# Hybrid retention and short-convolution block: token high and low parts side by side in 512-wide products, part sums by DMA, retention moved behind the input groups

## The chip, the cores and the metric

The kernel runs on one core of one Trainium2 chip. The metric is device time in microseconds (us), the median over several executions; less is better. One more execution was profiled: its trace gives the start and length of each instruction on each engine (TensorE, VectorE, ScalarE, GpSimd and SyncE; in the rows PE for matmuls, PEld for weight loads, DVE, ACT, POOL and SP), the DMA transfers, and the waits.

## The reference, cut to what matters

One layer over 512 tokens with 2048 features, float32:

```python
h = rmsnorm(x, norm_gain)
proj = h @ w_in                       # 2048 x 12288 columns
q, k, v, g_ret, c_b, c_c, c_x, g_conv, merge = split(proj)   # eight times 1024, then 4096
q = rotary(q); k = rotary(k) * 128 ** -0.5                   # 8 heads of 128
o = retention(q, k, v, decay, forward) + retention(q, k, v, decay, backward, strict)
branch_ret = o * rsqrt(mean(o * o) + eps) * gn_gain * silu(g_ret)
branch_conv = c_b * conv3_centred(c_c * c_x, conv_w) * silu(g_conv)
up = branch_ret @ w_branch[0], branch_conv @ w_branch[1]     # each 1024 x 2048
merged = sigmoid(merge[0]) * up[0] + sigmoid(merge[1]) * up[1]
out = rmsnorm(x + merged @ w_out, final_gain)
```

## The kernel before, in words

**Numbers in two parts.** Every float32 matrix is split in a rounded high part and the rest, the low part. `split_to` (L138) makes both: ScalarE copies to the high part (L140), VectorE subtracts (L141). A product is three matmuls (`mm3`, L143): high x high, high x low, low x high, each with its own weight load.

**Groups and pieces.** The columns of `w_in` are cut into 48 groups of 256: four each for k, q, v and g of the retention, 16 for the convolution, 16 for the merge gates. A group is four pieces of 512 KB (four k-tiles of 128 rows by 256 columns). `run` (L156) walks through all pieces in order: it issues the loads three pieces ahead on the SyncE queue, has the piece two ahead split, then emits the matmuls of the piece (`use`) and after that one entry of the list `background`. A piece has three `raw` buffers, three `whi` and two `wlo`, so the low part of piece n+2 can be written only when TensorE is through with piece n. The instructions of the first pieces are kept in program order; after `state["full"]` (L807) a scheduler that builds the program orders each engine's queue by its own estimates, and on the chip each queue then runs in that fixed order.

**Three kinds of input group.** `group` (L171) holds weights still and moves 512 tokens: 96 matmuls of 512 columns. `group_tok` (L277, for v) holds tokens still: 192 matmuls of 256 columns. `group_s` (L197) is a Strassen-Winograd form over 2 x 2 blocks (two halves of the tokens, two k-tiles, two column halves): seven products in place of eight, each of 256 tokens, 168 matmuls of 256 columns a group. Its weight sums are made on VectorE for each piece (`sums`, L134 to L136: one addition of 512 elements, two of 256), so that the pieces that are split have 1792 columns in place of 1024. Its token sums are made once (`token_forms`, L263). Its seven sums lie in four PSUM banks, and `combine` (L247) makes the four blocks from them: one ScalarE copy of 512 elements and four VectorE additions of 512. Two sets of four banks alternate.

**Order.** 12 plain groups and four of `group_tok` for the retention's k, q, v, g, pair of heads by pair of heads; the retention itself (`score`, `outp`, `rms_o`, `finish`) runs as background steps of later pieces, nine slots for a pair of heads. Then three plain gate groups, `token_forms`, 27 groups of `group_s` (16 of the convolution, 11 gates), two plain gate groups; then 16 groups of the two branch projections (1024 rows each, 48 matmuls of 512 columns), alternating, and the output projection. Gates and both branches go through DRAM on the GpSimd queue.

Of the kernel before, what the change touches and what calls it, by code (L numbers as in the profile page):

```python
# [20 lines left out]
H = 8  # L21
# [9 lines left out]
def hybrid_block_kernel(  # L31
# [20 lines left out]
    big = ctx.enter_context(tc.tile_pool(name="big", bufs=2))  # L52
    wp = ctx.enter_context(tc.tile_pool(name="wp", bufs=3))
    WF = 7 * 256
    dr = ctx.enter_context(tc.tile_pool(name="dr", bufs=1, space=bass.MemoryType.DRAM))
    ps = ctx.enter_context(tc.tile_pool(name="ps", bufs=2, space=PSUM))
# [13 lines left out]
    rsp = ctx.enter_context(ExitStack())  # L70
    gate_d = dr.tile([2, KT, P, S], F32, name="gate_d")
    ret_d = dr.tile([GG, P, S], F32, name="ret_d")
    conv_d = dr.tile([GG, P, S], F32, name="conv_d")

# [18 lines left out]
    state = {"loaded": 0, "split": 0, "used": 0, "full": False, "banks": 0}  # L93
# [6 lines left out]
    def load(pc, lo=0, hi=None):  # L100
        a, b = pc["dims"]
        if lo == 0:
            pc["F"] = wp.tile([P, WF], F32, name="raw", tag="raw", bufs=3)
            pc["raw"] = pc["F"][:, : a * b].rearrange("p (a b) -> p a b", a=a)
        pin(nc.sync.dma_start(out=pc["raw"][:, lo:hi], in_=pc["src"][:, lo:hi]))

    def split(pc, lo=0, hi=None):
        a, b = pc["dims"]
        if lo == 0:
            fl = []  # L110
            for n, k in (("whi", 3), ("wlo", 2)):
                if pc.get("last", 8) < 8 - k:
                    fl.append(fin["x"].tile([P, 1024], F32R, name=n, tag=n, bufs=8 - k))
                else:
                    fl.append(wp.tile([P, WF], F32R, name=n, tag=n, bufs=k))
# [8 lines left out]
    def blocks(pc):  # L124

        r = pc["F"][:, :1024].rearrange("p (r h c x) -> p r h c x", r=2, h=2, c=2)
        return r, pc["F"][:, 1024:].rearrange("p (f r x) -> p f r x", f=3, r=2)

    def sums(pc):

        r, s = blocks(pc)
        b21 = r[:, :, 1, 0, :].unsqueeze(2).broadcast_to([P, 2, 2, P])
        diag = pc["F"][:, :1024].rearrange("p (r m x) -> p r m x", r=2, m=4)[:, :, 0:4:3, :]
        nc.vector.tensor_tensor(s[:, 0:2].rearrange("p f r x -> p r f x"), diag, b21, op=ALU.add)  # L134
        nc.vector.tensor_tensor(r[:, :, 1, 0, :], s[:, 0], r[:, :, 1, 1, :], op=ALU.add)
        nc.vector.tensor_tensor(s[:, 2], r[:, :, 1, 0, :], r[:, :, 0, 1, :], op=ALU.add)  # L136
# [14 lines left out]
    def split_upto(n):  # L151
        while state["split"] < min(n, len(pieces)):
# [3 lines left out]
    def run(upto):  # L156
        while state["used"] < upto:
            i = state["used"]
            while state["loaded"] < min(i + 4, len(pieces)):
# [11 lines left out]
    def group(src, nk, rhs, post, mid=None):  # L171

        st = {}
        for q in range(nk // 4):
            def use(pc, q=q):
                if q == 0:
                    st["acc"] = ps.tile([P, 2, S], F32, name="acc", tag="acc")
                wh, wl = pc["w"]
                first = bool(mid) and q == 0
                for n in range(8):  # L180
# [3 lines left out]
                        mm3(  # L184
                            st["acc"][:, j, :],
                            (wh[:, k, c], wl[:, k, c]),
                            (rhs()[0][:, kt, :], rhs()[1][:, kt, :]),
                            kt == 0,
                            kt == nk - 1,
                        )  # L190
# [6 lines left out]
    def group_s(src, post):  # L197


        st = {}  # L200

        order = [
            (0, 0, "b11", "d4"), (0, 1, "b12", "a11"), (1, 1, "b22", "a12"), (2, 0, "v", "a1"),
            (1, 0, "u", "a22"), (3, 0, "z", "a7"), (3, 1, "w", "d6"),
        ]
        seen = [next(i for i, o in enumerate(order) if o[0] == b) for b in range(4)]
        for q in range(KT // 4):
            def use(pc, q=q):
                if q == 0:
                    pool = ps if state["banks"] % 2 == 0 else fin["psS"]  # L210
                    state["banks"] += 1
                    st["acc"] = [pool.tile([P, 2, S], F32, name="acc", tag="acc") for _ in range(2)]
                for n, (bank, half, b, a) in enumerate(order):
                    acc = st["acc"][bank // 2][:, bank % 2, half * 256 : half * 256 + 256]
                    for r in range(2):
                        mm3(
                            acc,
                            [weight_form(w, b, r) for w in pc["w"]],
                            token_form(a, 2 * q + r),
                            q == 0 and r == 0 and n in seen,  # L220
                            q == KT // 4 - 1 and r == 1,
                            skip_group_check=True,
                        )
                if q == KT // 4 - 1:
                    post(combine(*st["acc"]))
            pieces.append({"dims": (4, 256), "src": src[:, 4 * q : 4 * q + 4, :], "use": use, "forms": True})

    def weight_form(w, name, r):
        at = {"b11": 0, "b12": 128, "v": 256, "b22": 384}
        if name in at:  # L230
            o = 512 * r + at[name]
        else:
            o = 1024 + 256 * "uzw".index(name) + 128 * r
        return w[:, o : o + 128]

    def token_form(name, j):
        if name in ("a11", "a12", "a22"):
            kt, t = 2 * j + (name[2] == "2"), 256 * (name[1] == "2")
            return [h[:, kt, t : t + 256] for h in hT]
        i = ("d6", "d4", "a1", "a7").index(name)  # L240
        return [f[:, j, i, :] for f in part["forms"]]

    def swapped(t):

        return bass.AP(t.tensor, t.offset + 256, [t.ap[0], [-256, 2], [1, 256]])

    def combine(x, y):  # L247

        tp = part["tp"]
        t = tp.tile([P, 2, S], F32, name="T", tag="T", bufs=3)  # L250
        flat = t.rearrange("p j (i s) -> p (j i) s", i=2)
        s = tp.tile([P, S], F32, name="sc", tag="sc", bufs=1)
        nc.scalar.activation(s, x[:, 0, :], AF.Copy)
# [648 lines left out]
```

## Time and profile before

| | |
|---|---|
| median of 3 runs | 1443.73 us (1442.91 to 1446.1) |
| the profiled execution | 1444.66 us, of which the trace's span is 1442.8 us |
| TensorE busy | 1423.4 us, 99% of the span |
| VectorE busy | 945.2 us, 66% |
| ScalarE busy | 549.2 us, 38% |
| DMA | 174.93 MB, mean 121 GB/s |
| mean granted TensorE clock | 0.995 of full speed |

Busy time of TensorE is the time in which at least one matmul is under way; matmuls overlap, so the distance between starts, not the length of one, says how fast it goes. An engine's mean share is taken over stages of different kinds, so the stages are read one by one.

### The profile page before, as it was taken

Reading aid. Unit: us, or ns where it says so; the run is one execution under the profiler, and the core shown is the slowest. Engines: PE = TensorE matmul, PEld = TensorE weight load, DVE = VectorE, ACT = ScalarE, POOL = GpSimd, SP = SyncE. Lnnn points to the kernel's source line nnn. Section 1 sums busy time; section 2 is a strip of 40 time slices with the busy share of each in tenths; the row PEclk is TensorE's granted clock in tenths of the full one; section 3 lists DMA queues with packets and bytes.
Section 4 is the critical chain, followed back from the end, with each engine's and each line's share of the span. In section 5 each row is a group of like instructions: output and inputs, shape, how many; then the busy total and the mean of one; then the engine's idle time right before and its main releaser. Section 6 shows DMA issues by size and latency. Waiting matters only on the chain.

```text
span 1442.8 us, 20988 instructions
## 1 busy us (share of the span) xinstructions
PE 1423.4 (99%) x8810; PEld 1286.1 (89%) x8810; DVE 945.2 (66%) x1220; ACT 549.2 (38%) x586; POOL 65.8 (5%) x80
## 2 busy tenths in 40 slices
PE   8999999999999999999999999999999999999997
PEld 7888988988988899999999999999978888888886
DVE  4846557466467989988898899889643444522433
ACT  6435335354344434443344334434342222222421
POOL 0000000000000000000000000000010000201210
PEclk9999999999999999999999999999999999999999
DMA  6322322322323333443344334433464444543412
GB/s 229 94 87 84 107 77 86 102 79 97 102 68 121 117 95 106 140 132 103 103 132 135 100 116 134 132 103 103 148 231 161 146 146 146 186 179 102 162 55 105
DMA packets 140610, 174.93 MB, mean 121 GB/s; under 512 B 5940, under 2 KB 122724, under 8 KB 139876
## 3 DMA queue, kind: packets, MB, share of 16 engines
q1 hardware_dynamic: 132788, 143.17, 30.7%
q0 software_dynamic: 7696, 30.41, 6.3%
q8 instruction: 69, 1.13, 0.3%
q14 instruction: 25, 0.20, 0.0%
q10 hardware_dynamic: 32, 0.01, 0.0%
HBM read 156.79 MB, written 16.78 MB: 120 GB/s over the span
## 4 chain that ended last, share of the span: by engine, by line
PE 92%; DVE 5%; DMA 2%; issue 1%; ACT 0%; SPq 0%; DVEq 0%; ACTq 0%
PE acc L147 29%; PE acc L145 29%; PE acc L146 29%; DVE wlo L141 2%; DMA raw<-in_w_in_dram 1%; PE op L147 1%; PE sp L147 1%; PE sp L145 1%; PE op L145 1%; PE op L146 1%; PE sp L146 1%; DVE raw L134 0%; PE xtp L346 0%; DMA xb<-in_x_dram 0%; DVE fl L141 0%
## 5 line engine op out<-in xcount | busy, mean ns | idle before, releaser
L141 DVE TENSOR_TENSOR wlo<-raw,whi 128x1024 fp32r<-128x1024 f32 (+2 forms) x257 | 402.5, 1568 | 351.0 <-PE acc L147 139.8
L140 ACT ACTIVATE whi<-raw 128x1024 fp32r<-128x1024 f32 (+2 forms) x257 | 339.6, 1326 | 560.1 <-PE acc L146 312.9
L147 PE MATMUL acc<-hTh,wlo 128*128 128x256 f32 (+1 forms) x1192 | 396.0, 332 | 2.4 <-DVE wlo L141 2.4
L145 PE MATMUL acc<-hTh,whi 128*128 128x256 f32 (+1 forms) x1192 | 396.6, 333 | 0.7 <-DVE de L257 0.7
L146 PE MATMUL acc<-hTl,whi 128*128 128x256 f32 (+1 forms) x1192 | 395.9, 332 | 0.0
L147 PEld LDWEIGHTS acc<-hTh,wlo 128*128 128x128 f32 x1192 | 227.0, 190 | 24.9 <-DVE wlo L141 3.3
L147 PE MATMUL acc<-fh,wlo 128*128 128x256 f32 x864 | 245.5, 284 | 2.6 <-DVE wlo L141 2.6
L145 PEld LDWEIGHTS acc<-hTh,whi 128*128 128x128 f32 x1192 | 227.2, 191 | 22.1 <-issue 0.8
L146 PEld LDWEIGHTS acc<-hTl,whi 128*128 128x128 f32 x1192 | 227.1, 191 | 21.2
L145 PE MATMUL acc<-fh,whi 128*128 128x256 f32 x864 | 244.6, 283 | 0.3 <-DVE T L574 0.2
L146 PE MATMUL acc<-fl,whi 128*128 128x256 f32 x864 | 244.5, 283 | 0.0
L147 PEld LDWEIGHTS acc<-fh,wlo 128*128 128x128 f32 x864 | 166.1, 192 | 3.6 <-DVE wlo L141 3.3
L145 PEld LDWEIGHTS acc<-fh,whi 128*128 128x128 f32 x864 | 166.0, 192 | 0.8 <-DVE T L574 0.4
L146 PEld LDWEIGHTS acc<-fl,whi 128*128 128x128 f32 x864 | 166.0, 192 | 0.0
L146 PE MATMUL acc<-wlo,mTh 128*128 128x512 f32 (+1 forms) x272 | 102.5, 377 | 0.0
L147 PE MATMUL acc<-whi,mTl 128*128 128x512 f32 (+1 forms) x272 | 102.5, 377 | 0.0
L145 PE MATMUL acc<-whi,mTh 128*128 128x512 f32 (+1 forms) x272 | 102.5, 377 | 0.0
L145 PE MATMUL acc<-bh,whi 128*128 128x512 f32 x256 | 99.6, 389 | 0.0
L146 PE MATMUL acc<-bl,whi 128*128 128x512 f32 x256 | 99.6, 389 | 0.0
L147 PE MATMUL acc<-bh,wlo 128*128 128x512 f32 x256 | 99.6, 389 | 0.0
L134 DVE TENSOR_TENSOR raw<-raw 128x512 f32<-128x512 f32 x108 | 74.3, 688 | 16.4 <-DMA raw<-in_w_in_dram 16.3
L146 PE MATMUL acc<-wlo,hTh 128*128 128x256 f32 x256 | 72.4, 283 | 0.0
(171 smaller groups left out, 1546.0 us busy)
## 6 DMA issues: line engine op xcount, KB each, us to landing
raw<-in_w_in_dram SPq DMA_DIRECT2D x191, 512.0 KB, 3.6
raw<-in_w_branch_dram SPq DMA_DIRECT2D x32, 512.0 KB, 3.3
raw<-in_w_out_dram SPq DMA_DIRECT2D x32, 512.0 KB, 3.6
gate_d<-T POOLq DMA_DIRECT2D x16, 512.0 KB, 3.8
gl<-gate_d POOLq DMA_DIRECT2D x16, 512.0 KB, 4.4
y<-in_x_dram POOLq DMA_DIRECT2D x4, 1024.0 KB, 6.6
xb<-in_x_dram SPq DMA_DIRECT2D x12, 256.0 KB, 6.4
ret_d<-tmp POOLq DMA_DIRECT2D x8, 256.0 KB, 2.4
```

The source lines that it names most:

```text
L134: nc.vector.tensor_tensor(s[:, 0:2].rearrange("p f r x -> p r f x"), diag, b21, op=ALU.add)
L140: pin(nc.scalar.activation(hi, src, AF.Copy))
L141: pin(nc.vector.tensor_tensor(lo, src, hi.bitcast(F32), op=ALU.subtract))
L145: pin(nc.tensor.matmul(acc, lh, rh, start=start, stop=False, **kw))
L146: pin(nc.tensor.matmul(acc, lh, rl, start=False, stop=False, **kw))
L147: pin(nc.tensor.matmul(acc, ll, rh, start=False, stop=stop, **kw))
```

## The change

- 40 of the 48 input groups use `group_s`: all but the four of k and the four of v. So 13 groups that were plain (four q, four g, five gates) join the 27.
- In a product of `group_s` the high and low parts of the tokens lie side by side: one matmul moves both (512 columns) under the high part of the weights, a second one of 256 columns adds the weights' low part times the tokens' high part. Each product has a PSUM bank of its own, in two halves. In the last piece of a group ScalarE copies each of the seven banks to SBUF (`ev`, one buffer); a DMA on the GpSimd queue then adds the second halves onto the first, and `combine` takes its four additions from there.
- For this the tokens h are stored as three arrays: k-tiles 0 to 7 (`h1`), and k-tiles 8 to 15 in halves of 256 tokens (`h00`, `h10`). Plain groups therefore use two matmuls of 256 for k-tiles 8 to 15. `h10` is written to DRAM before the `group_s` stage, its place is taken by `ev`, and it is read back for the last two v groups.
- Order: k (four groups), v 0 and 1, token forms in the background of these; the 40 groups; then the projections of the convolution branch, with v 2 and 3 among them, with the whole retention as background in 22 slots (27 steps; in five slots two steps come together); then the projections of the retention branch. q, k, v, g and the gated projection of the convolution branch go through DRAM.

```diff
-    order = [(0, 0, "b11", "d4"), (0, 1, "b12", "a11"), (1, 1, "b22", "a12"), ...]
+    order = [
+        ("b11", "d4", 0), ("b12", "a11", 1), ("u", "a22", 2), ("b22", "a12", 3),
+        ("z", "a7", 4), ("w", "d6", 5), ("v", "a1", 6),
+    ]
     for q in range(KT // 4):
         def use(pc, q=q):
             if q == 0:
-                st["acc"] = [pool.tile([P, 2, S], F32, name="acc", tag="acc") for _ in range(2)]
+                tiles = [fin["p7"].tile([P, 2, 256], F32, name="acc", tag="acc") for _ in order]
+                st["acc"] = tiles if state["banks"] else [tiles[i] for i in (4, 5, 6, 2, 3, 0, 1)]
...
                 for r in range(2):
-                    mm3(acc, [weight_form(w, b, r) for w in pc["w"]], token_form(a, 2 * q + r), ...)
+                    wh, wl = [weight_form(w, b, r) for w in pc["w"]]
+                    x = token_form(a, q + 4 * r)
+                    first, last = q == 0 and r == 0, q == KT // 4 - 1 and r == 1
+                    nc.tensor.matmul(acc, wh, x, start=first, stop=False, skip_group_check=True)
+                    nc.tensor.matmul(acc[:, 1, :], wl, x[:, 0], start=False, stop=last, skip_group_check=True)
+                if q == KT // 4 - 1:
+                    nc.scalar.activation(EV()[:, :, place, :], acc, AF.Copy)
             if q == KT // 4 - 1:
-                post(combine(*st["acc"]))
+                sum_parts()
+                if pc.get("defer"):
+                    state["defer"] = lambda: post(combine())
+                else:
+                    post(combine())
+
+def sum_parts():
+    e = EV()
+    nc.gpsimd.dma_start(out=e[:, 0, 0:7, :], in_=e[:, 1, 0:7, :], accum_op=ALU.add)
...
+def combine():
+    e = EV()[:, 0]
+    t = T()
+    flat = t.rearrange("p j (i s) -> p (j i) s", i=2)
+    s, back = e[:, 0:2, :], e[:, 3, :]
+    back = bass.AP(back.tensor, back.offset, [back.ap[0], [-256, 2], [1, 256]])
+    nc.vector.tensor_tensor(flat[:, 1:3, :], s, e[:, 2:4, :], op=ALU.add)
+    nc.vector.tensor_tensor(s, s, back, op=ALU.subtract)
+    m1 = e[:, 6:7, :].broadcast_to([P, 2, 256])
+    nc.vector.tensor_tensor(s, s, m1, op=ALU.add)
+    nc.vector.tensor_tensor(flat[:, 0:4:3, :], s, e[:, 4:6, :], op=ALU.add)
...
 def group(src, nk, rhs, post, mid=None, ahead=None):
...
+                    for t, r in rhs(kt):
+                        mm3(st["acc"][:, j, t : t + r.shape[2]], (wh[:, k, c], wl[:, k, c]), (r[:, 0], r[:, 1]), ...)
...
+others = [(cols(0, i), rotary_post(q_d, i)) for i in range(4)] + [(cols(3 * BW, i), g_post(i)) for i in range(4)]
+others += [(cols(8 * BW, i), gate_post(i)) for i in list(range(8, 16)) + list(range(8))]
 for i in range(BW // 256):
+    for n, (off, post) in enumerate(conv_posts(i)):
+        group_s(cols((4 + off) * BW, i), post)
+        for _ in range((1, 2, 1, 2)[n]):
+            group_s(*others.pop(0))
...
+for n in range(2):
+    up_group(1, n, conv_up_post(n))
+for i in range(2, 4):
+    group_tok(cols(2 * BW, i), v_post(i))
+    up_group(1, i, conv_up_post(i))
+for i in range(4, 8):
+    up_group(1, i, conv_up_post(i))
+n_r = len(pieces)
 for i in range(D // 256):
+    up_group(0, i, ret_up_post(i))
...
+def retention_program():
+    steps = [[] for _ in range(6 * (H // 2) + 3)]
+    for i in range(H // 2):
+        a, b = 2 * i, 2 * i + 1
+        own = [
+            [L(split_v, i), L(split_head, a), L(decay_table, a), L(fetch_head, b)],
+            [L(score, a, 0), L(score, a, 1)],
+            [L(outp, a, 0), L(outp, a, 1), L(score, a, 2), L(score, a, 3), L(fetch_g, a)],
+            [L(outp, a, 2), L(outp, a, 3), L(square, a), L(split_head, b), L(decay_table, b)],
+            [L(score, b, 0), L(score, b, 1), L(rms_o, a)] + ([L(fetch, i + 1), L(fetch_head, a + 2)] if b + 1 < H else []),
+            [L(outp, b, 0), L(outp, b, 1), L(score, b, 2), L(score, b, 3), L(finish, a), L(fetch_g, b)],
+            [L(outp, b, 2), L(outp, b, 3), L(square, b)],
+            [L(rms_o, b)],
+            [L(finish, b)],
+        ]
+        for k, s in enumerate(own):
+            steps[6 * i + k] += s
+    n = 22
+    return [sum(steps[k * len(steps) // n : (k + 1) * len(steps) // n], []) for k in range(n)]
```

`rotary_post`, `g_post` and `v_post` now end in a write to DRAM; `fetch`, `fetch_head` and `fetch_g` read it back into SBUF on the GpSimd queue, `split_head` and `split_v` split it there. The piece of a `group_s` group now takes k-tiles q, q+4, q+8 and q+12, and the token forms lie in four arrays by q, so that each comes free after the piece that uses it last. The load and the split of the convolution branch's tokens stand at the end of the 40 groups, those of the retention branch's after the retention.

## Rows read from the trace of the kernel before

**Rows 1.** The page's first part: busy time, share of the span, instructions.

```profile
PE 1423.4 (99%) x8810; PEld 1286.1 (89%) x8810; DVE 945.2 (66%) x1220; ACT 549.2 (38%) x586; POOL 65.8 (5%) x80
```

**Rows 2.** Busy time by stretch: length, PE, PEld, DVE, ACT, POOL, clock, DMA share, GB/s.

```profile
40.00:240.00 200.00, 200.00 (x1063) 172.65 (x1062) 120.85 (x195) 87.65 (x111) 1.83 (x3) 1.00 0.28 88
240.00:440.00 200.00, 200.00 (x1061) 172.85 (x1060) 112.50 (x150) 85.73 (x110) 2.16 (x4) 1.00 0.28 88
700.00:860.00 160.00, 159.31 (x1325) 158.91 (x1324) 141.21 (x174) 63.52 (x46) 2.85 (x4) 1.00 0.37 116
```

**Rows 3.** The same view of the passage into the `group_s` stage.

```profile
490.00:500.00 10.00, 8.03 (x63) 7.41 (x61) 9.97 (x14) 5.31 (x5) 0.71 (x1) 1.00 0.31 105
500.00:510.00 10.00, 9.93 (x70) 9.93 (x71) 8.39 (x12) 3.41 (x2) 0.00 (x0) 0.83 0.38 115
```

**Rows 4.** Timelines of PE: start, length, matmul; first and last of 53 and 20.

```profile
899.75 0.28 PE L146 MATMUL acc<-fl,whi 128*128 128x256 f32 x1
...
905.99 0.28 PE L147 MATMUL acc<-fh,wlo 128*128 128x256 f32 x1
...
1149.65 0.39 PE L145 MATMUL acc<-bh,whi 128*128 128x512 f32 x1
...
1153.95 0.39 PE L146 MATMUL acc<-bl,whi 128*128 128x512 f32 x1
```

**Rows 5.** Timeline of DVE at a `group_s` group's end: start, length, instruction.

```profile
572.37 0.68 DVE L255 TENSOR_TENSOR T<-sc,acc 128x512 f32<-128x512 f32 x1
572.96 2.02 DVE L141 TENSOR_TENSOR wlo<-raw,whi 128x1792 fp32r<-128x1792 f32 x1
574.90 0.68 DVE L257 TENSOR_TENSOR de<-sc,acc 128x512 f32<-128x512 f32 x1
575.50 0.69 DVE L134 TENSOR_TENSOR raw<-raw 128x512 f32<-128x512 f32 x1
...
576.70 0.42 DVE L135 TENSOR_TENSOR raw<-raw 128x256 f32<-128x256 f32 x1
577.03 0.68 DVE L260 TENSOR_TENSOR T<-de,acc 128x512 f32<-128x512 f32 x1
...
579.57 1.22 DVE L612 TENSOR_TENSOR T<-T,rsrow 128x1024 f32<-128x1024 f32 x1
580.70 0.42 DVE L136 TENSOR_TENSOR raw<-raw 128x256 f32<-128x256 f32 x1
```

**Rows 6.** Groups of instructions, 560 to 860 us: busy, mean; idle before.

```profile
L141 DVE TENSOR_TENSOR wlo<-raw,whi 128x1792 fp32r<-128x1792 f32 x60 | 121.1, 2022 | 16.4 <-PE acc L147 13.8 <-ACT whi L140 2.2
...
L140 ACT ACTIVATE whi<-raw 128x1792 fp32r<-128x1792 f32 x60 | 101.3, 1700 | 106.9 <-DVE raw L136 66.1 <-PE acc L146 35.3 <-PE acc L147 5.5
L253 ACT ACTIVATE sc<-acc 128x512 f32<-128x512 f32 x15 | 8.8, 588 | 15.5 <-PE acc L147 15.5
```

**Rows 7.** DMA issues: size of one, median us to landing.

```profile
gate_d<-T POOLq DMA_DIRECT2D x16, 512.0 KB, 3.8
...
y<-in_x_dram POOLq DMA_DIRECT2D x4, 1024.0 KB, 6.6
```

**Rows 8.** Waits in all (total, times, longest); DVE's timeline where the branches load.

```profile
ACT bh L140 <- DMA bl<-conv_d: 9.5, 4, 3.2
...
1076.83 1.23 DVE L141 TENSOR_TENSOR bl<-bl,bh 128x1024 fp32r<-128x1024 f32 x1 [1.80 <-ACT bh L140]
1077.97 2.35 DVE L141 TENSOR_TENSOR wlo<-raw,whi 128x1024 fp32r<-128x1024 f32 x2
```

**Rows 9.** Timelines of DVE and ACT: what follows two scores.

```profile
92.29 1.28 DVE L481 SCALAR_TENSOR_TENSOR tmp<-sp,tb 128x512 f32<-128x512 f32 x2
93.67 1.29 DVE L141 TENSOR_TENSOR sl<-tmp,sh 128x512 fp32r<-128x512 f32 x2
...
93.01 1.23 ACT L140 ACTIVATE sh<-tmp 128x512 fp32r<-128x512 f32 x2 [0.97 <-DVE tmp L481]
```

**Rows 10.** Groups by line and shape, 40 to 440 us, DVE: one of rotary's three.

```profile
L425 DVE TENSOR_TENSOR tmp<-acc,rot 128x512 f32<-128x512 f32 x16 | 11.0, 690 | 6.4 <-ACT tmp L423 6.4
```

More of the change, by code (lines that the diff above doesn't have):

```diff
@@ L92, in hybrid_block_kernel @@
     fin = {}
-    state = {"loaded": 0, "split": 0, "used": 0, "full": False, "banks": 0}
+    state = {"loaded": 0, "split": 0, "used": 0, "full": False, "banks": 0, "limit": 0}
     def pin(ins):
@@ L151, in split_upto @@
     def split_upto(n):
-        while state["split"] < min(n, len(pieces)):
+        while state["split"] < min(n, state["limit"]):
             split(pieces[state["split"]])
@@ L158, in run @@
             i = state["used"]
-            while state["loaded"] < min(i + 4, len(pieces)):
+            while state["loaded"] < min(i + 4, state["limit"]):
                 load(pieces[state["loaded"]])
@@ L176, in use @@
                 if q == 0:
[L177 removed]
+                    st["acc"] = acc_tile()
+                    if ahead:
+                        ahead()
                 wh, wl = pc["w"]
@@ L846, in hybrid_block_kernel @@
-    mT.append(big.tile([P, KT, S], F32R, name="mTl", tag="big"))
+    ps_x.__exit__(None, None, None)
+    xst.close()
+    for z in range(2):
+        nc.gpsimd.dma_start(out=a21_d[z].rearrange("j p s -> p j s"), in_=hold["h10"][:, z])
+    fms = ExitStack()
+    fm = [
+        fms.enter_context(tc.tile_pool(name=f"fm{i}", bufs=1, side="right", reuse_waits="tile")).tile(
+            [P, 2, 2, 4, 256], F32R, name="fm"
+        )
+        for i in (3, 2, 1, 0)
+    ]
+    part["forms"] = fm[::-1]
@@ new lines, in hybrid_block_kernel @@
+    for j in range(KT // 2):
+        background.extend([[lambda j=j: token_forms(j)], []])
+    run(n_a)
+    while background:
+        for f in background.pop(0):
+            f()
+    psx.close()
+    h10x.close()
+    with tc.tile_pool(name="p7", bufs=8, space=PSUM) as p7:
+        fin["p7"] = p7
+        lr = ctx.enter_context(tc.tile_pool(name="lr", bufs=1, reuse_waits="tile"))
+        fin["ev"] = lr.tile([P, 2, 7, 256], F32, name="ev", tag="h10", padded_shape=[P, 2, 8, 256])
+        run(n_s)
@@ new lines, in hybrid_block_kernel @@
+    for _ in range(3):
+        load(pieces[state["loaded"]])
+        state["loaded"] += 1
+    for i in range(4):
+        load_branch(1, i)
+    split_upto(n_s + 2)
+    state["defer"]()
+    rsx.close()
+    hold["h10"] = lr.tile([P, 2, KT // 2, 256], F32R, name="h10", tag="h10")
+    for z in range(2):
+        nc.gpsimd.dma_start(out=hold["h10"][:, z], in_=a21_d[z].rearrange("j p s -> p j s"))
+    ret = ExitStack()
+    rps["sb"] = ret.enter_context(tc.tile_pool(name="ret", bufs=2, side="right", reuse_waits="tile"))
@@ new lines, in hybrid_block_kernel @@
+    rps["p"] = ret.enter_context(tc.tile_pool(name="rps", bufs=2, space=PSUM))
+    dist = rps["dist"] = rps["sb"].tile([P, TW], F32, name="dist", bufs=1)
+    ones = rps["ones"] = rps["sb"].tile([P, P], F32R, name="ones", bufs=1)
+    nc.vector.tensor_copy(ones, onesf)
+    nc.gpsimd.iota(dist, pattern=[[1, TW]], base=-OFF, channel_multiplier=-1, allow_small_or_imprecise_dtypes=True)
+    fetch(0)
+    fetch_head(0)
+    background.extend(retention_program())
+    run(n_r - 2)
+    while background:
+        for f in background.pop(0):
+            f()
@@ new lines, in hybrid_block_kernel @@
+    br0 = rps["br0"] = big.tile([P, 2, GG, S], F32R, name="br0", tag="h1")
+    brs[0] = lambda kt: [(0, br0[:, :, kt, :])]
+    rps["stg"] = big.tile([P, 2, 2, 2, S], F32, name="stg", tag="h00")
+    for i in range(2):
+        load_merge(i)
+    for i in range(4):
+        load_branch(0, i)
+    run(n_r)
+    ret.close()
+    bbx.close()
+    mp = ctx.enter_context(tc.tile_pool(name="mp", bufs=1, side="right", reuse_waits="tile"))
+    mTb = mp.tile([P, 2, KT, S], F32R, name="mT")
+    mT.extend([mTb[:, 0], mTb[:, 1]])
```

492 lines of the change are left out of this document (232 added, 260 removed).

## The prediction

> **What bounds the kernel now.** I read the page's first part, then the stages one by one, then the distance between starts on TensorE and VectorE, then the waits. TensorE is busy 99% of the span [rows 1], and in the two long stages shown it does not stand: 200 of 200 us while the retention runs, 159.31 of 160 in the `group_s` stage [rows 2]. So each column and each weight change less on TensorE shows in the time, as long as nothing else becomes late. VectorE is the engine that could: only 66% over the span [rows 1], but 141 of 160 us in the `group_s` stage [rows 2], where each piece has 1792 columns to split and three additions to make first.
>
> What a matmul costs is the distance of starts: 6.24 us over 52 steps with 256 columns, 0.120 us each; 4.30 us over 19 steps with 512, 0.2263 us [rows 4]. At 2.4 GHz (the full granted clock, [rows 2]) 256 columns alone are 0.107 us and 512 are 0.213, so each matmul carries 0.013 us beside its columns, whatever its width. That is what a wider product saves.
>
> **The change part by part.**
>
> *Side by side.* A product and k-tile was three matmuls of 256, 0.360 us; it becomes one of 512 and one of 256, 0.346. A group has 56 of these: 20.16 us before, 19.39 after. For the 27 groups there are, 27 x 0.77 = 20.7 us less. Two weight loads in place of three are under the matmuls as before.
>
> *Thirteen more groups.* A plain group is 96 x 0.2263 = 21.72 us, so 13 x (21.72 - 19.39) = 30.3 us less.
>
> *The four k groups* now move k-tiles 8 to 15 as two matmuls of 256: 48 x (0.240 - 0.2263) = 0.66 us a group, 2.6 us more. v keeps 192 x 0.120 = 23.04 us; projections and retention keep their matmuls. TensorE's sum: -20.7 - 30.3 + 2.6 = **-48.4 us**.
>
> *VectorE under the 40 groups.* From start to start a 512-wide step costs 0.60 us, a 256-wide one 0.33, the subtraction of 1792 columns 1.94, a 1024-wide step 1.13 [rows 5]. A piece: 0.60 + 2 x 0.33 + 1.94 = 3.2, a group 12.8, `combine` still four steps, 2.4. What follows (gates one wide step; q three; g one wide and two 512; the four convolution groups together about 10.3 us) is 82 us over the 40 groups, 2.1 a group. That makes 17.3 of 19.4 us, 89%, and 2.1 us free; before it was 17.2 of 20.16, 3.0 free, with 0.7 us of TensorE idle in 160 [rows 2]. So VectorE hides still, with a third less room. In the first ten groups (four q, two g, a convolution block) it is about 18.1 of 19.4.
>
> *ScalarE.* One copy of 512 becomes seven, 7 x 0.59 = 4.1 us a group beside 4 x 1.70 for the high parts [rows 6] and 1 to 2 for the rest: 13 of 19.4, free. In the last piece a copy waits for its product, which ends every 2 x 0.346 = 0.69 us; behind it in the queue stands at most the next high part, due a piece (4.85 us) later. Seven banks of eight are used, and the next group's n-th product takes a bank whose copy was made several products before: I cost that at nothing.
>
> *The sum by DMA.* 896 KB are added onto 896 KB, on the GpSimd queue. No row of before has such a transfer. Below, it is a plain one: 512 KB land in 3.8 us and 1024 KB in 6.6 [rows 7], so 896 KB in 5.9. Above, the bytes count twice: on the same line 1792 KB take 10.8. I take 7.5, nearer to the 1024 KB row. With t the end of a group's matmuls, the last copy ends at t + 0.6 and the sum lands at t + 8.1. Until then VectorE has the low part of the piece after next (from t, when TensorE frees its buffer), sums for two further pieces, and from t + 4.85 the next low part to t + 6.8: little standing, if they are ahead of `combine` in the queue. `ev` is one buffer: it must be read by t + 19.39 - 4.2 = t + 15.2, when the next group's first copy comes; that holds for a landing time up to 15.2 - 0.6 - 2.4 = 12.2 us, above both bounds. Behind the sum on GpSimd's queue are only this group's own writes. The order shown in [rows 5] (a subtraction of a later piece between the steps of `combine`) says that the queue is mixed by an estimate, not left in program order. I take 5 us in all for standing in this stage (0 to 10 in this case).
>
> Beside that row stands a rule. The Trainium skill's page "Collectives: The Full Stack", section "The bandwidth ceiling: the fold count and why AG ≠ RS ≠ AR", says that an add inside a DMA is slow because it reads two sources through one ring, not because of the addition, and halves the rate. No transfer here shows it; by it the sum would be at the 10.8 end, VectorE would wait until t + 11.4, and the room before t + 15.2 would be 1.4 us in place of 4.7.
>
> *Token forms moved.* In the passage into the stage TensorE was idle 1.97 us in 10, and the next 10 us had a mean granted clock of 0.83, so a third of them at 1.2 GHz after that standing, 1.7 us lost [rows 3]. Now the forms are made under k and v groups, where VectorE is about 60% busy [rows 2]: -3.7 us.
>
> *Start.* The eight last k-tiles are converted as two halves: 0.33 x 2 against 0.60 on VectorE and about the same on ScalarE by [rows 5]; 0 to 4 us, I take 2.
>
> *Retention moved.* Its matmuls (8 x 26 x 0.2263 = 47 us) go between 24 pieces of the convolution branch and of v: 16 x 5.43 + 8 x 5.76 + 47 = 180 us. VectorE: 233 us in the two stretches of [rows 2], less 64 splits of 1.13, less rotary (48 steps of 0.69 [rows 10], 33 us), less about 15 for v and g: 113 for the retention, and 36 wide steps (41 us) for splits, gating and loaded tokens: 154 of 180. It hides, but with less room than before. A chain from score to the split ready for `outp` is 2.7 us ([rows 9]: 92.29 to 94.96). With a slot each it was hidden (200 of 200 us); in the five double slots it may be bare: 0 to 5 x 2.7 = 13 us, I take 6. Heads now come from DRAM; each fetch is issued two slots (about 15 us) ahead of a 3.8 us transfer.
>
> *Passages.* At the end of the 40 groups the last two token tiles of the convolution branch are split only when the token forms are free, about 1.1 + 1.1 us under a first piece of 5.4: -2 to 4 us (before, this passage stood too, rival 1), I take 1. The last head has its finish (3.0 us of VectorE), a write and a load (3.8 each by [rows 7]), its normalising and a split ahead of it, some 16 us, covered by two pieces and what comes ahead of its k-tile, 17.6: 0 to 5, I take 3.
>
> **Sum:** -48.4 - 3.7 + 5 + 2 + 6 + 1 + 3 = -35.1 us against the profiled 1444.66 (span 1442.8 and 1.9 around it): 1409.6. That execution lies 0.9 above the median, so 1408.7; I say **1409**. With all unknowns at their lower ends about 1390, at their upper ends 1428.
>
> **The rivals.**
>
> 1. *Slower: VectorE stands at `combine`.* Queues run in their built order. If the sum lands later than the order assumes, VectorE stands at `combine`'s first step, and behind it are the weight sums and low parts of the next pieces, for which TensorE waits after two pieces. Before has this in small: a split of loaded tokens waits up to 3.2 us for its DMA, VectorE stands 1.80 us behind that, and the low part of the next piece comes only then [rows 8]. Free are 2.1 us a group, so s us of standing cost 40 x (s - 2.1); all other terms give -40, so it decides from s = 3.1 us on. At 4.5 us it is 96 us: about 1500, with lower clock in the pauses as in [rows 3]. For it: the one unknown transfer and the thin room. Against: small steps, two pieces of lead, and a queue that is mixed. Chance 0.17. By the page's rule named above s would be up to 3.3 us longer than with my 7.5, if the order did not count on it.
>
> 2. *Half of it is eaten.* VectorE stands 2.3 to 3 us a group, or runs full in the retention stage (169 of 180 if the 15 us for v and g are none), and TensorE pauses a little in many places: 1428 to 1441. Chance 0.13.
>
> 3. *Side by side saves nothing.* If a moving operand in two separate runs costs a matmul's extra for each run, the pair is 0.360 like the triple, and only 13 x 1.56 - 2.6 = 17.7 us of the 48.4 remain: 1440. Against: the extra of 0.013 us is per matmul in both widths [rows 4]. Chance 0.03. The Trainium skill, "TensorE: Matmul & The Clock Gate", section "Back-to-back issue gap", has an extra of only about 2.5 ns beside the columns; by it the two forms would differ by 2.5 ns a product, TensorE's sum would be -36 us and the time 1421; the rows of this case, 0.120 and 0.2263, are against it.
>
> **How the numbers follow.** My forecast has 0.62 (1390 to 1428). Rivals 2 and 3 are faster too: 0.78 together. Rival 1 has 0.17. What lies between, s near 3.1 and within 0.2% (2.9 us, about what a measurement of this kernel can tell from no change), 0.05. The range that leaves out 2 in 10 goes from 1391 to 1442.
>
> **What would show it.** Right: starts 0.346 us apart for each pair, 19.4 us a group, TensorE without gaps over some 776 us; the sum's landing between 5.9 and 10.8 us; VectorE's waits for `ev` under 2 us a group; 180 us from the end of the 40 groups to the second branch. Wrong: waits of VectorE on the sum of over 3 us, of ScalarE's copies on `combine` (the one buffer), of TensorE on low parts in each group, a granted clock under 1 in that stage; pairs 0.36 apart; gaps of TensorE at double slots.

## The result and the profile after

The changed kernel takes **1544.59 us** (median of 4 runs, 1538.24 to 1549.31) against 1443.38 before on the same chip: ratio 1.0694, interval 1.0652 to 1.0737. It is 101 us slower, where 35 us less was forecast. The profiled execution took 1542.84 us, its span is 1541.1. One execution of one kernel of the experiments (`combine` forced behind the next low part) took 4870.71 us, for no cause that the record shows, and is left out of its numbers below.

The page's first part, then busy time by stretch (length, PE, PEld, DVE, ACT, POOL, granted clock, DMA share, GB/s): the stage with 40 `group_s` groups, its end, and the retention.

```profile
PE 1424.6 (92%) x7698; PEld 1219.0 (79%) x7698; DVE 1080.0 (70%) x1412; ACT 699.8 (45%) x828; POOL 142.3 (9%) x184
...
200.00:1000.00 800.00, 723.00 (x3923) 617.03 (x3923) 629.77 (x778) 389.87 (x420) 47.83 (x59) 0.97 0.55 148
1065.00:1100.00 35.00, 24.93 (x101) 19.23 (x100) 17.82 (x19) 15.57 (x20) 11.60 (x17) 0.90 0.96 275
1095.00:1100.00 5.00, 0.45 (x1) 0.45 (x2) 2.30 (x3) 4.83 (x6) 2.23 (x4) 0.65 0.86 283
1100.00:1150.00 50.00, 49.26 (x300) 43.97 (x300) 43.66 (x63) 31.35 (x45) 9.69 (x18) 0.97 0.55 184
1150.00:1200.00 50.00, 49.48 (x306) 43.99 (x305) 38.49 (x55) 31.20 (x42) 10.58 (x16) 1.00 0.52 178
```

TensorE, 99% busy before [rows 1], now stands 77 of 800 us in the stage, where it stood 0.7 of 160 [rows 2]; its granted clock averages 0.97 of 2.4 GHz there. The period of a group follows from the instructions on `ev` (duration min/median/max, first and last start):

```profile
L263 POOL DMA_DIRECT2D ev<-ev x40: 832/864/919, 177.7 to 1068.0; - x40
...
DMA to landing us min/median/max: 6.3/8.0/10.0
```

(1068.0 - 177.7) / 39 = 22.83 us a group, where 19.39 was forecast; over 40 groups that is 138 us, the whole miss of 136. The waits say who is late (us in total, times, longest):

```profile
DVE T L286 <- DMA ev<-ev: 121.3, 38, 5.4
PEld acc L245 <- DVE wlo L161: 103.7, 59, 3.8
PE acc L245 <- DVE wlo L161: 84.4, 53, 3.4
...
DVE raw L154 <- DMA raw<-in_w_in_dram: 54.2, 51, 3.9
```

L286 is `combine`'s first step. VectorE stands there in 38 of 40 groups, and TensorE then stands for low parts (L161). VectorE's timeline shows what is queued behind the waiting step:

```profile
501.67 2.02 DVE L161 TENSOR_TENSOR wlo<-raw,whi 128x1792 fp32r<-128x1792 f32 x1
...
506.24 0.69 DVE L286 TENSOR_TENSOR T<-ev 128x512 f32<-128x512 f32 x1 [2.55 <-DMA ev<-ev]
506.85 0.42 DVE L155 TENSOR_TENSOR raw<-raw 128x256 f32<-128x256 f32 x1
...
528.62 0.69 DVE L286 TENSOR_TENSOR T<-ev 128x512 f32<-128x512 f32 x1 [3.15 <-DMA ev<-ev]
```

The second and third additions of a weight piece (L155, L156) come behind `combine`, and with them its split and the release of its buffer. The chain of work that ended last (start, length, what) shows how a sum and the loads follow each other:

```profile
497.80 8.41 DMA ev<-ev
...
511.48 1.93 DVE wlo L161
513.41 0.03 DVE raw L156
513.44 5.00 DMA raw<-in_w_in_dram
...
522.04 8.03 DMA raw<-in_w_in_dram
```

The load at 522.04, which runs beside the next sum, takes 8.03 us where the median is 4.3. It lands at 530.07; VectorE has stood for the sum until 528.62, so most of that delay passes while it stands anyway. TensorE itself works as forecast. Its timeline has pairs of one 512 and one 256 at:

```profile
504.18 0.40 PE L244 MATMUL acc<-fm,whi 128*128 128x512 f32 x1
504.42 0.28 PE L245 MATMUL acc<-fm,wlo 128*128 128x256 f32 x1
504.53 0.39 PE L244 MATMUL acc<-fm,whi 128*128 128x512 f32 x1
```

504.53 - 504.18 = 0.35 us; 32 pairs between 500.01 and 511.13 give 0.3475 (forecast 0.346; three 256 took 0.360 [rows 4]).

### The profile page after: what moved, and what is told of

The parts are those of the page before. It is cut to its first block, busy times and chain, and to the rows that moved or that the text cites. A ratio compares the mean times of both kernels' runs of the same rounds, so it can differ in the third digit from the quotient of the medians.

```text
span 1541.1 us, 19513 instructions
## 1 busy us (share of the span) xinstructions
PE 1424.6 (92%) x7698; PEld 1219.0 (79%) x7698; DVE 1080.0 (70%) x1412; ACT 699.8 (45%) x828; POOL 142.3 (9%) x184
## 4 chain that ended last, share of the span: by engine, by line
PE 25%; DMA 16%; DVE 16%; issue 8%; ACT 4%; POOL 0%; DVEq 0%; ACTq 0%; POOLq 0%; SPq 0%
DMA ev<-ev 8%; PE acc L166 7%; PE acc L165 7%; PE acc L167 7%; DMA raw<-in_w_in_dram 7%; DVE wlo L161 6%; DVE raw L154 2%; ACT ev L247 2%; ACT whi L160 1%; DVE T L290 1%; DVE ev L289 1%; PE acc L244 1%; DVE ev L287 1%; DVE T L642 1%; DVE raw L155 1%
## 5 line engine op out<-in xcount | busy, mean ns | idle before, releaser
L160 ACT ACTIVATE whi<-raw 128x1792 fp32r<-128x1792 f32 (+2 forms) x257 | 372.5, 1459 | 537.6 <-DVE raw L156 283.4
L161 DVE TENSOR_TENSOR wlo<-raw,whi 128x1792 fp32r<-128x1792 f32 (+2 forms) x257 | 441.3, 1719 | 161.6 <-PE acc L166 59.4
L244 PE MATMUL acc<-fm,whi 128*128 128x512 f32 x1280 | 462.0, 399 | 4.0 <-ACT T L483 1.7
L245 PE MATMUL acc<-fm,wlo 128*128 128x256 f32 x1280 | 366.4, 287 | 84.8 <-DVE wlo L161 84.4
L244 PE MATMUL acc<-h,whi 128*128 128x512 f32 x960 | 362.0, 411 | 0.0
L245 PEld LDWEIGHTS acc<-fm,wlo 128*128 128x128 f32 x1280 | 244.4, 191 | 104.3 <-DVE wlo L161 103.7
L244 PEld LDWEIGHTS acc<-fm,whi 128*128 128x128 f32 x1280 | 243.5, 190 | 59.7 <-ACT whi L160 2.8
L245 PE MATMUL acc<-h,wlo 128*128 128x256 f32 x960 | 276.7, 290 | 0.0
L244 PEld LDWEIGHTS acc<-h,whi 128*128 128x128 f32 x960 | 190.9, 199 | 44.6
L154 DVE TENSOR_TENSOR raw<-raw 128x512 f32<-128x512 f32 x160 | 109.6, 686 | 54.6 <-DMA raw<-in_w_in_dram 54.2
L286 DVE TENSOR_TENSOR T<-ev 128x512 f32<-128x512 f32 x40 | 27.7, 692 | 121.3 <-DMA ev<-ev 121.3
L165 PE MATMUL acc<-whi,mT 128*128 128x512 f32 (+1 forms) x272 | 103.0, 379 | 0.0
L167 PE MATMUL acc<-whi,mT 128*128 128x512 f32 (+1 forms) x272 | 102.1, 375 | 0.0
L156 DVE TENSOR_TENSOR raw<-raw 128x256 f32<-128x256 f32 x160 | 67.1, 421 | 2.7
L155 DVE TENSOR_TENSOR raw<-raw 128x256 f32<-128x256 f32 x160 | 67.0, 420 | 2.4
```

Of the source, the lines that this page charges most:

```text
L155: nc.vector.tensor_tensor(b21, s[:, 1], b22, op=ALU.add)
L156: nc.vector.tensor_tensor(s[:, 2], b21, b12, op=ALU.add)
L160: pin(nc.scalar.activation(hi, src, AF.Copy))
L161: pin(nc.vector.tensor_tensor(lo, src, hi.bitcast(F32), op=ALU.subtract))
L165: pin(nc.tensor.matmul(acc, lh, rh, start=start, stop=False, **kw))
L167: pin(nc.tensor.matmul(acc, ll, rh, start=False, stop=stop, **kw))
```

## The experiments

Theory after reading the trace: rival 1, VectorE stands at `combine` for the sum. Its rivals: the sum's bytes make the weight loads late, and the wide products do not deliver. The table gives medians where there are several runs. Kernels whose ratio is given ran four times; the others ran once, and four executions of one kernel here lie 2 to 13 us apart, so a few us between single ones say little. Kernels named "aside" sum into the second half of `ev`, which `combine` does not read.

**1. The sum taken apart: its wait, its bytes, its addition.**

```diff
-        nc.gpsimd.dma_start(out=e[:, 0, 0:7, :], in_=e[:, 1, 0:7, :], accum_op=ALU.add)
+        pass                                                                   # no sum
+        nc.gpsimd.dma_start(out=e[:, 1, 0:7, :], in_=e[:, 1, 0:7, :], accum_op=ALU.add)  # sum aside
+        nc.gpsimd.dma_start(out=e[:, 1, 0:7, :], in_=e[:, 1, 0:7, :])          # plain copy aside
+        nc.gpsimd.dma_start(out=e[:, 0, 0:7, :], in_=e[:, 1, 0:7, :])          # plain copy, waited for
```

No sum. 

> The changed kernel without the DMA that adds the second halves of the seven banks onto the first (so the low parts of the tokens are missing from the 40 groups); the seven copies, the banks and the order stay. Standing (VectorE stands in its queue at the first step of combine until the sum has landed, 3.0 us a group, and the weight sums behind it come too late): 1400 to 1430 us, 19.4 to 20 us a group. Traffic (the bytes of the sum make the weight loads late): the same, 1400 to 1430. Work (seven copies on ScalarE and 17.3 us of VectorE a group are too much by themselves): 1500 or more.

Sum aside. 

> The changed kernel with a sum of the same size that adds the second halves onto themselves, so that combine, which reads the first halves alone, need not wait for it (the low parts of the tokens are missing from the 40 groups); the bytes on the DMA engines stay. Standing: 1405 to 1435 us, no wait of VectorE on the sum, and weight loads as late as in the changed kernel. Traffic: 1500 or more, with VectorE's waits for weights at 54 us or above. Work: 1500 or more.

Plain copy aside. 

> The changed kernel with the sum's transfer as a plain copy of the second half of ev onto itself, with no addition: as many bytes are written, nothing is added, nothing waits for it (the low parts are missing from the 40 groups' results). Theory: what makes weight loads late is the time the transfer takes on the 16 DMA engines. If the addition counts (two sources read), the copy lands in 5.5 to 7 us rather than 8.7 and the time is 1430 to 1445, between the 1416 without any transfer and the 1457 with the adding one. Rival: an adding transfer and a plain one load the engines alike, and the time is 1450 to 1465 with a landing of 8 to 9.

Plain copy, waited for. 

> The changed kernel with a plain copy of the low parts over the high parts in place of the addition (so that the results of the 40 groups are wrong), and combine waiting for it in its old place. With a landing of 6.2 in place of 8.0 us VectorE waits some 1.8 us less in each group: 121 - 72 = 50 us of waits. Theory that wait and late loads add up: the wait's 86 us shrink to 30 or 40, the traffic's 41 to 8, so 1455 to 1470. Rival, that standing at that place costs as much whatever the landing: 1500 to 1520.

| transfer of 896 KB | `combine` waits | us | wait for `ev` | waits for weights | landing |
|---|---|---|---|---|---|
| none | no | 1416.17 | - | 49.1 | - |
| plain | no | 1423.86 | - | 54.9 | 6.2 |
| plain | yes | 1453.41 | 44.0 | 49.4 | 5.4 |
| adding | no | 1457.34 | - | 95.1 | 8.7 |
| adding (the change) | yes | 1544.59 | 121.3 | 54.2 | 8.0 |

Standing and Traffic both forecast the first kernel; the one with the sum aside falls between their ranges, so neither alone is right; the two plain copies come out 6 and 2 us under the ranges of their theories. With neither wait nor bytes the kernel is near the forecast: TensorE is busy 692.89 of 700 us in the stage, and its waits for low parts are 7.2 us in place of 84.4. First the changed kernel's wide matmuls (the last two times are the first and the last start), then three rows of the kernel without a sum:

```profile
L244 PE MATMUL acc<-fm,whi x1280: 388/395/633, 152.6 to 1065.9; 128*128 128x512 f32 x183
```

```profile
L244 PE MATMUL acc<-fm,whi x1280: 387/395/497, 153.0 to 944.9; 128*128 128x512 f32 x183
...
200.00:900.00 700.00, 692.89 (x3958) 601.93 (x3957) 639.23 (x784) 391.46 (x423) 17.85 (x25) 1.00 0.40 125
...
PE acc L245 <- DVE wlo L161: 7.2, 9, 2.5
```

The 40 groups take 791.9 us without the sum, 19.8 a group, and 913.3 with it. So the side-by-side product does on TensorE what it says, and nearly all that is lost is in the sum: 121 us in this stage.

Waiting costs 1453.41 - 1423.86 = 30 us with a plain copy and 87 with an adding one; the addition costs 1457.34 - 1423.86 = 33 us where nothing waits and 91 where VectorE does. Together the sum costs 128 us, more than 30 + 41, but this does not show that wait and traffic make each other worse: the adding transfer lands later, so VectorE stands 121.3 us for it in place of 44.0, and each us of standing costs 0.7 us in both (30 / 44.0 and 87 / 121.3). In the change itself the weights are hardly later than without a sum (waits 54.2 against 49.1): the 121 us of the stage match the 121.3 us of standing at `combine`. The late loads (95.1) come out where nothing waits for the sum.

That an addition loads the DMA more than a copy, the GpSimd queue's part of the DMA table shows (packets, MB, share of the span of 16 engines). No sum, then plain copy aside, then sum aside:

```profile
q0 software_dynamic: 18960, 59.78, 12.6%
```

```profile
q0 software_dynamic: 24720, 96.48, 19.0%
...
raw<-in_w_in_dram SPq DMA_DIRECT2D x191, 512.0 KB, 4.2
ev<-ev POOLq DMA_DIRECT2D x40, 896.0 KB, 6.2
```

```profile
q0 software_dynamic: 24720, 96.48, 25.1%
...
raw<-in_w_in_dram SPq DMA_DIRECT2D x191, 512.0 KB, 4.4
ev<-ev POOLq DMA_DIRECT2D x40, 896.0 KB, 8.7
```

Times the spans (1414.2, 1422.1, 1455.3 us) these are 178, 270 and 365 us of all 16 engines. By difference, the plain copy takes 92 / 40 = 2.3 us for each of 40 transfers, the adding one 187 / 40 = 4.7, for the same packets and bytes; this takes the queue's other transfers as alike in all three, as the weight loads are, whose own queue takes 454 to 459 us in each. The rule quoted in the forecast (the Trainium skill, "Collectives: The Full Stack", section "The bandwidth ceiling: the fold count and why AG ≠ RS ≠ AR": the add halves the rate), which the page states for the reduce step of a collective, agrees with that pair of numbers. The cause that it names, two reads through one ring, no run here separates. The landing grew less: 8.0 us, not the 10.8 that the forecast worked out by it.

**2. The wait moved.** First by program order: `combine` emitted behind the next group's first or second piece.

```diff
-                        post(combine())
+                        state["late"] = lambda: post(combine())
+                elif q == 0 and "late" in state:      # second kernel: q == 1
+                    state.pop("late")()
```

> The changed kernel with combine and what follows it emitted after the first piece of the next group in place of directly behind the sum; all work and all bytes stay. Standing: the weight sums come ahead of it in VectorE's queue, its wait on the sum falls from 3.0 us a group to under 1, time 1415 to 1460 us. Traffic: 1530 to 1550, as the bytes stay. Work: 1530 to 1550.

> As the run before, but after the second piece of the next group. Standing: wait on the sum near 0, time 1405 to 1450 us, unless ScalarE's copies of the next group now wait for the one buffer ev. Traffic and work: 1530 to 1550.

1539.41 (ratio 1.0677, 1.0661 to 1.0693) and 1547.94 (1.0721, 1.0678 to 1.0765), waits for `ev` 121.1 and 122.5 us: the queue is ordered by the builder's own estimates, and emitting later left the wait as it was. So neither run tests Standing. Then by force, behind the low part of the piece four after the group's last (`wlo` is the last low part emitted):

```diff
+                elif q == 1 and "late" in state:
+                    with tc.issue_after(state["wlo"].ins):
+                        state.pop("late")()
```

> The changed kernel with combine forced, in VectorE's queue, behind the low part of the piece that is four after the group's last one (one low part later than it stands now); moving it in the program text alone left the queue's order as it was, 1539 and 1548 us. Standing: the wait on the sum falls from 3.0 us a group to under 0.5, the time to that of the run with the sum aside, 1445 to 1475 us. Traffic: 1530 to 1550. If the single buffer ev becomes the new wait, ScalarE's copies wait for combine and the time is between.

1513.35 (1.0484, 1.0467 to 1.0502), between the two ranges, but not because of the one buffer: ScalarE's copies wait 6.5 us in all for `combine`. The wait moved rather than went:

```profile
DVE raw L155 <- DMA raw<-in_w_in_dram: 129.7, 69, 6.7
...
DVE T L291 <- DMA ev<-ev: 15.3, 13, 4.7
```

VectorE now stands for weights whose loads run beside the sum. Three kernels ask whether it is the order, any transfer, or the addition; all have `combine` at that late place.

> Combine stands behind the next group's low part, as in the run that cost 1513, and the sum writes its own source, so that no step of VectorE waits for it; the bytes still move (the low parts are missing from the 40 groups' results). Theory A: the new order itself is what costs there, since combine's steps now delay the sums of a piece whose weights then stand in their buffer longer and the next load starts later. Then the time stays at about 1510 (1500 to 1520) and VectorE still waits some 110 to 130 us for weights. Theory B: what is left of the wait for the sum (15 us) and what queues behind it costs there. Then it falls to the 1457 of the kernel with the sum aside and combine in its old place (1450 to 1470), with some 95 us of waits for weights.

> The same order, and no sum at all (the low parts are missing from the 40 groups' results). If the traffic of the sum and the order add up, the time is some 41 us under that of the run before it in this list, as 1416 is under 1457 with combine in its old place. If the order costs only because loads are slow beside the sum's traffic (theory C), it comes down to 1416 (1410 to 1425). If the order costs by itself (theory A), it stays at 1450 to 1475.

> Combine behind the next low part, three buffers for loaded weights, the transfer a plain copy of the second half of ev onto itself (nothing is added, nothing waits for it; low parts missing from the 40 groups' results). Theory: what makes loads late is the longer time of an adding transfer on the DMA engines. Then the time is 1425 to 1440, against 1509 with the adding one and 1423 without any. Rival, any 896 KB at that place does it: 1480 to 1510.

Sum aside 1509.4 (waits for weights 143.4), no sum 1423.0, plain copy 1439.67 (69.2). So the late place costs 7 us by itself, 16 beside a plain copy and 52 beside an adding one, each against the same transfer with `combine` in its old place, and each between single executions, so that 7 and 16 are not far from the spread. Theory A's range holds beside the sum and C's without it: the order costs because loads are slow beside the adding transfer. My reading, which no run tests by itself: with nothing to wait for at the old place, `combine`'s four steps fill the time in which the loads are slow, and at the late place VectorE stands for the loads first and does those steps afterwards.

Then a fourth buffer for loaded weights, paid with the third one for high parts, in the stages before the retention:

```diff
-  name="raw", tag="raw", bufs=3
+  name="raw", tag="raw", bufs=pools.get("raws", 4)
-  state["loaded"] < min(i + 4, ...)
+  state["loaded"] < min(i + 1 + pools.get("raws", 4), ...)
-  tag=n, bufs=k
+  tag=n, bufs=k if "WF" in pools else 2
```

> Combine behind the next group's low part, the sum by DMA as changed, and in the stages before the retention four buffers for loaded weights (loads issued one piece earlier) and two in place of three for the high parts; it computes all. Theory (a ring: VectorE's low part frees the buffer, the load starts, VectorE waits for it): the waits for weights fall from 130 us to under 40 and the time from 1513 to 1430 to 1455. Rival (adding transfers slow the loads however early they start, or two buffers for high parts are too few): 1490 to 1520.

> Combine behind the next low part, the sum writing its own source (low parts missing from the 40 groups' results, nothing waits for it), and the same four buffers for loaded weights. Theory of the ring: 1425 to 1440, against 1509 with three. Rival: 1490 to 1515.

> The changed kernel with the same buffers (four for loaded weights, two for high parts), combine in its old place; it computes all. Theory: the wait at combine (121 us) stays, the waits for weights (54 us) go: 1490 to 1515. Rival, the wait alone sets the pace: 1535 to 1550.

Late `combine`: 1482.41 (1.0282, 1.0265 to 1.0299) with the sum, 1477.88 with it aside; waits for weights 108.5 and 116.2. Both theories were half right: loads issued a piece earlier give back 31 us, and the kernel with the sum aside is still 38 us above the top of the 1425 to 1440 that a ring alone would give. In its old place: 1550.28, waits for `ev` 78.1, for low parts on TensorE 90.3; no gain, against my theory and at the top of the rival's range. From 200 to 900 us VectorE's waits for ScalarE's high parts show a new cost, first in the changed kernel, then with the four buffers:

```profile
DVE wlo L161 <- ACT whi L160: 7.7, 10, 1.4
```

```profile
DVE wlo L161 <- ACT whi L160: 61.2, 47, 3.4
```

ScalarE in turn waits 197.8 us there for matmuls of TensorE (18.0 in the changed kernel). That points at the two buffers for high parts; four buffers for loaded weights with three for high parts were not tried.

**3. Other ways to add.**

```diff
# two sums
+                        if place == 3:
+                            sum_parts(0, 4)
-                    sum_parts()
+                    sum_parts(4, 7)
# on GpSimd
+        nc.gpsimd.tensor_tensor(e[:, 0, 0:7, :], e[:, 0, 0:7, :], e[:, 1, 0:7, :], op=ALU.add)
# four of seven: places 4 to 6 as three matmuls, the sum behind the fourth copy
+                        if place == 3:
+                            sum_parts()
+        nc.gpsimd.dma_start(out=e[:, 0, 0:4, :], in_=e[:, 1, 0:4, :], accum_op=ALU.add)
```

Two sums. 

> The changed kernel with the sum in two DMAs: four banks (512 KB) issued as soon as the fourth copy is made, some 2 us sooner, and three banks (384 KB) at the end. Standing: if combine stays where it is in VectorE's queue, it waits 2 to 4 us a group less and the time falls to 1450 to 1490 us; if the builder of the queues moves combine ahead by what it expects to gain, the wait stays at about 3 us a group and the time at 1530 or above. Traffic: 1530 to 1550, the bytes are the same.

On GpSimd. 

> The changed kernel with the sum made by one addition of 1792 elements on GpSimd in place of the DMA. By GpSimd's row of 512 elements in 1.63 us it takes 5.7 us, against 8.0 for the DMA, and puts no bytes on the DMA engines. Standing: 1420 to 1460 us if VectorE's own instructions do not get longer. Traffic: 1415 to 1430. If GpSimd and VectorE slow each other, VectorE's 512-wide steps are longer than 0.69 us and the time is 1480 or more.

Four of seven. 

> The first four of the seven products side by side, copied out as two parts and summed by one DMA of 512 KB behind the fourth copy; the other three as three matmuls of 256, one part copied out. It computes all. Against the kernel with three matmuls everywhere (1432) TensorE saves 4 x 8 x 0.0137 = 0.44 us a group, 18 us; the sum starts about 2 us before the group's end and lands in about 5.4. If traffic costs in proportion (41 us for 896 KB) and the wait is small, it costs 23 us and some of a wait: 1435 to 1460. If the wait for its landing comes back as in the kernel with two sums (64 us of waits on the first), it is 1470 to 1500. If a small transfer hides in full: 1414 to 1420, better than the three matmuls.

Two sums: 1507.46, between the ranges; the halves land in 5.4 and 6.8 us, the waits are 64.3 and 24.0. On GpSimd: 1548.33 (1.0733, 1.0715 to 1.0751), with a wait of 12.1 us for the sum, but VectorE's own steps grew. By line in the stage (busy, mean ns):

```profile
L263 POOL TENSOR_TENSOR ev<-ev 128x1792 f32<-128x1792 f32 x35 | 152.7, 4362 | 378.8 <-ACT ev L247 302.2 <-DVE raw L154 76.6
...
L154 DVE TENSOR_TENSOR raw<-raw 128x512 f32<-128x512 f32 x138 | 115.4, 840 | 26.1 <-DMA raw<-in_w_in_dram 25.9
L155 DVE TENSOR_TENSOR raw<-raw 128x256 f32<-128x256 f32 x138 | 107.3, 783 | 2.1
```

In the changed kernel L154 and L155 take 686 and 420 ns. Here they are 154 and 363 longer on the mean, in steps that read two operands from SBUF while GpSimd reads two. "SBUF — State Buffer" of the Trainium skill, section "Who interferes with whom", says that such a pair shares a read port; the case agrees with that. Four of seven: 1492.34 (1.0337, 1.0316 to 1.0359), waits for `ev` 63.6: a transfer of 512 KB, issued two microseconds before the end of a group, does not hide either.

**4. All of the change but the side-by-side product.**

```diff
-   nc.tensor.matmul(acc, wh, x, ...)
-   nc.tensor.matmul(acc[:, 1, :], wl, x[:, 0], ...)
+   mm3(acc[:, 0, :], (wh, wl), (x[:, 0], x[:, 1]), first, last, skip_group_check=True)
-   nc.scalar.activation(EV()[:, :, place, :], acc, AF.Copy)
+   nc.scalar.activation(EV()[:, 0, place, :], acc[:, 0, :], AF.Copy)
-   nc.gpsimd.dma_start(out=e[:, 0, 0:7, :], in_=e[:, 1, 0:7, :], accum_op=ALU.add)
```

> All of the change but the side-by-side form: three matmuls of 256 into one half of each bank, copies of 256 columns, no sum by DMA; the result is complete. TensorE needs 20.16 us a group in place of 19.4. Standing and traffic: 1416 (the run without the sum) plus 30: 1435 to 1455 us. Work: 1500 or more.

And the same with the four buffers. 

> Control: three matmuls of 256 and no sum, with the same buffers; it computes all. By theory its small waits for weights (37 us in all) hardly reach TensorE, so the time is 1428 to 1434, as with three buffers (1432); if two buffers for high parts are too few, it is over 1440.

1432.31 (0.9923, 0.9898 to 0.9947) and **1428.59 (0.9904, 0.9889 to 0.9918)**. Both are faster than the kernel before and the changed one, by 0.8 and 1.0% of the kernel before; the first is 3 us under its range. In the second the stage has no gap of TensorE at all:

```profile
200.00:900.00 700.00, 700.00 (x5874) 700.00 (x5873) 632.35 (x779) 355.27 (x422) 17.17 (x24) 1.00 0.40 124
```

So all of the change but the wide product, thirteen more groups and the moved retention in it, is worth 10 us (1442.43 to 1432.31), 14 with four buffers; the side-by-side product with its sum costs 112 (1432.31 to 1544.59). Even without the sum it saves only 1432.31 - 1416.17 = 16 us (one execution), half of the 40 x 0.77 = 31 that TensorE's sum had: VectorE's steps and its waits for weights then fill 669 of the 700 us from 200 to 900 (639.23 and 29.8).

## Why the prediction was wrong

**The step that failed** is *The sum by DMA*: "little standing, if they are ahead of `combine` in the queue" and "I take 5 us in all for standing in this stage (0 to 10 in this case)". The landing was sized well (8.0 us against 7.5, between the bounds 5.9 and 10.8). Three things were not.

- *The condition about the queue did not hold.* Weight additions of coming pieces stand behind `combine`. VectorE waits 121 us, not 5, and [rows 8] had shown the pattern. This is rival 1, which had 0.17.
- *The room that was to take up the wait was hardly there.* "Free are 2.1 us a group" prices the measured s = 3.0 us at 40 x 0.9 = 36 us in place of the 5, some 1440 and not 1545. VectorE's busy time is 629.77 / 800 x 22.83 = 18.0 us a group, not 17.3, and without any sum it still waits 49.1 / 40 = 1.2 us a group for weights: 0.2 of 19.4 us are left. With them the price is 40 x 2.8 = 112 us, near the 121 by which the stage grew. [rows 2] had it: 141.21 of 160 us are 17.8 in 20.16, where the forecast took 17.2.
- *The bytes were given no price on the weight loads.* The transfer was costed as a landing time only. By the difference above it holds the 16 DMA engines 4.7 us of each group, and the loads of weights, which start only when VectorE has freed a buffer, land later. Where nothing waits for the sum this is 41 us (1416 to 1457); in the change it passes for the most part behind the standing, but a kernel rid of the standing alone, the one with the sum aside, is still slower than the one before.

**Right:** a pair at 0.346 (rival 3 is out); seven banks, seven copies and one `ev` without a stall of their own (ScalarE 390 of 800 us); the sum's landing; TensorE in the retention nearly full, 49.26 and 49.48 of 50 us from 1100 to 1200.

**Off in size:** *Passages*, taken at 1 + 3 us. The way into the projections shows TensorE busy 0.45 of 5 us (first fence) and ScalarE waiting for a load that runs beside the refill of `h10`, with the DMA engines 96% busy from 1065 to 1100 us:

```profile
1095.14 1.06 ACT L160 ACTIVATE whi<-raw 128x1024 fp32r<-128x1024 f32 x1 [10.14 <-DMA raw<-in_w_in_dram]
```

From 1065 to 1100 TensorE is busy 24.93 of 35 us, so 10 us are idle (4 in the kernel without a sum). From the last wide matmul of the 40 groups to the first matmul of the second branch are 200 us (193 without a sum), where the forecast had 180 and some 10 for standing. *Thirteen more groups* and *side by side*: without a sum the 40 groups run at 19.8 against 19.39, some 16 us more, of which the 5 for standing were in the forecast. As that kernel ends 7 us above the forecast, the terms left came out some 4 us better together than I summed them; which of them was not tried.

**Still open:** why with a fourth buffer the late `combine` stays 59 us above the same place without a sum (1482.41 against 1423.0), and how much of the 101 us is the lower clock after TensorE's pauses (mean 0.97 in the stage).

## What to carry to other kernels

A transfer that feeds an in-order engine has two prices: its landing time at the place where the engine waits, and the time it takes from other transfers on the same DMA engines; cost both. They need not add up: while the engine stands for the one transfer, the others catch up, and their price shows only when the standing is gone. Before calling an engine's spare time free, subtract the waits it already has. What one engine saves must be larger than what the saving asks of the others: 0.77 us a group of TensorE here cost 896 KB of adding transfers.

## What the runs showed of the hardware

By the difference between the kernels, an adding DMA from SBUF to SBUF kept the 16 DMA engines busy twice as long as a plain copy of the same 896 KB (4.7 against 2.3 us), and it landed 2.5 us later (8.7 against 6.2). A GpSimd addition of 1792 columns (4.4 us) lengthened VectorE's 256-column additions from 420 to 783 ns on the mean. The instruction that issues an adding transfer holds GpSimd 0.86 us, a plain one 0.56.
